# Five of eight pairs by seven products, with TensorE's matmuls in program order

## The chip, the cores and the metric

The kernel runs on one core of a Trainium2 chip. The metric is device time in microseconds, the median of several runs. The core's engines are TensorE (PE, matmuls; its weight loads are listed apart as PEld), VectorE (DVE), ScalarE (ACT) and GpSimd (POOL); SyncE (SP) issues the DMAs. Each engine takes its instructions in the order of its own queue and waits on semaphores for the others.

## The reference

A two-layer encoder trunk on x of 256 tokens by 2048 channels, in float32. Each layer is a mixer followed by a feed-forward part:

```python
x = layer_norm(DN_ALPHA * x + y, ln_mix_g[layer], ln_mix_b[layer])       # y from the layer's mixer
f = swiglu(x, ffn_w_gate[layer], ffn_w_up[layer], ffn_w_down[layer])
x = layer_norm(DN_ALPHA * x + f, ln_ffn_g[layer], ln_ffn_b[layer])

def swiglu(x, w_gate, w_up, w_down):
    return (jax.nn.silu(x @ w_gate) * (x @ w_up)) @ w_down
```

`w_gate` and `w_up` are 2048 x 5632, `w_down` is 5632 x 2048. The mixers (neighbourhood attention with a gated recurrence in layer 0, pooling with grouped-query attention in layer 1) are outside the change.

## The kernel before

**Numbers in two parts.** A float32 value is held as `hi`, rounded to the matmul's type float32r, and `lo`, the rest. `split` (L121) makes both: ScalarE casts (L122), VectorE subtracts (L123). `mm3` (L289) multiplies two such pairs by three matmuls (lo by hi, hi by hi, hi by lo) of 128x128 weights and 512 columns; the activations are the weights that are loaded, the split weight matrix streams. Tokens make two blocks of 128, the 2048 channels 16 blocks of 128.

**Loads.** `load_half` (L147) brings 512 KB of a weight matrix as `raw` and splits it into `whi` and `wlo`; in the stretch of the change there are four rooms of each. These loads have the planner's priority moved ahead by 400 instructions, so that they are made early.

**The feed-forward part.** `ffn` (L546) treats the 5632 hidden channels as 11 chunks of 512. Chunks 0 and 1 are done by `whole`. The other nine are units, nine calls of `unit` (L463) in each of the two layers, arranged in rounds:

```python
ROUNDS = (((2, 3), (0, 1)), ((4, 5), (2, 3)), ((6, 7), (4, 5)), ((8, 9), (6, 7)), ((10,), (8,)))
```

In the round ((4, 5), (2, 3)), the units 4 and 5 make gate and up of their chunks, while pieces of the down projection of chunks 2 and 3, made a round earlier, run between their products. `down_steps` (L516) is a generator, and each `next` is one piece: one half load of `w_down` and 12 matmuls into `acc`. For each of four column blocks n, the pieces go through the chunks of the round: first chunk half 0, half 1, second chunk half 0, half 1. A round of two units has 16 pieces, 8 per unit. Chunks 9 and 10 have their down projection at the layer's end.

**Seven products.** A unit computes [gate, up] for the two token blocks. Of the 16 channel blocks two neighbours form a pair p, so that a pair is a 2x2 by 2x2 block product, with 8 products done plainly. The pairs in `SEVEN` are done with 7, by Winograd's form of Strassen's method. It needs sums of blocks: those of x (`e`, `f`, `g`, `h` in `fm`) are made once a layer by `forms_of` (L417), in steps handed out by `make` (L584) after the half loads of chunk 1; those of the weights for every pair in `load_seven` (L441), which loads 1024 KB as `rs`, adds on VectorE into `z` (L452 to L454), casts and subtracts into `sh`, `sl` (four planes, two rooms) and `zh`, `zl` (one plane more, four rooms, kept until the second half of the unit). There is one room of `z` and two of `rs`.

A unit begins with two down pieces; then it transposes the two token blocks of the previous unit's y (`flips`, which call `transpose4`, L274: four transposes by TensorE, then a split into `yTh`, `yTl`, of which there are four rooms). Then come the pairs of `SEVEN`, four products each into the banks c11, c12, c22, c21, with down pieces after each by `GAPS`; a few additions on the banks (L482 to L487); and in the second half, by turns, the remaining three products of a pair in `SEVEN` and the eight of a pair in `PLAIN`. At the end silu(gate) times up makes `g`, whose transposes the next unit does. The banks `un` are a ring of four that serves the transposes and the four results.

**The order.** A planner arranges each engine's queue by the data's dependences, by the priority of program order and by a simulated time line. Splits of y and the last steps have a priority moved ahead by 1000, loads by 400. A matmul passed through `tc.keep_in_program_order` (in `mm3` with `pin`) is tied behind the TensorE instruction traced before it; in units and down pieces no matmul is.

Of the kernel before, what the change touches and what calls it, by code (L numbers as in the profile page):

```python
# [71 lines left out]
LAST = (9, 10)  # L72
SEVEN = (4, 5, 6, 7)
PLAIN = (0, 1, 2, 3)
GAPS = (2, 1, 1, 2)


@with_exitstack
def trunk(ctx: ExitStack, tc: tile.TileContext, a, out):
# [177 lines left out]
    def new_yT():  # L257
        yh = ap_.tile([P, 4, T], F32R, tag="yTh", name="yTh", bufs=4)
        yl = ap_.tile([P, 4, T], F32R, tag="yTl", name="yTl", bufs=4)
        return yh, yl  # L260

    def x_lhs(xT):
# [153 lines left out]

    def forms_of(sp, xT, out):  # L417

        n = len(SEVEN)
        xs = sp.tile([P, NT, 2 * n, P], F32, tag="rs", name="xs", bufs=2)  # L420
        fs = sp.tile([P, 4, n, P], F32, tag="z", name="fs", bufs=1)
        yield
        for t in range(NT):
            s = slice(2 * SEVEN[0], 2 * SEVEN[0] + 2 * n)
            nc.vector.tensor_tensor(xs[:, t], xT[0][t][:, s, :].bitcast(F32), xT[1][t][:, s, :].bitcast(F32), op=add)
            yield
        x11, x12, x21, x22 = (xs[:, t, e : 2 * n : 2, :] for t in range(2) for e in range(2))
        e, f, g, h = (fs[:, i] for i in range(4))
        nc.vector.tensor_tensor(e, x22, x21, op=sub)
        nc.vector.tensor_tensor(f, e, x11, op=add)  # L430
        yield
        nc.vector.tensor_tensor(g, x11, x21, op=sub)
        nc.vector.tensor_tensor(h, x12, f, op=sub)
        yield
        hi, lo = split_tile(sp, [P, 4, n, P], fs, "fm")
        for i, p in enumerate(SEVEN):
            x = lambda t, k: (xT[0][t][:, k, :], xT[1][t][:, k, :])
            e, f, g, h = (at((hi, lo), slice(None), j, i) for j in range(4))
            out[p] = {"11": x(0, 2 * p), "12": x(0, 2 * p + 1), "22": x(1, 2 * p + 1), "e": e, "f": f, "g": g, "h": h}

    def load_seven(sp, src):  # L441

        with tc.high_priority(offset=400):
            raw = sp.tile([P, 4, NCH], F32, tag="rs", name="rs", bufs=2)
            hi = sp.tile([P, 4, NCH], F32R, tag="sh", name="sh", bufs=2)
            lo = sp.tile([P, 4, NCH], F32R, tag="sl", name="sl", bufs=2)
            zh = sp.tile([P, NCH], F32R, tag="zh", name="zh", bufs=4)
            zl = sp.tile([P, NCH], F32R, tag="zl", name="zl", bufs=4)
            z = sp.tile([P, 4, NCH], F32, tag="z", name="z", bufs=1)
# [13 lines left out]
    def unit(sp, w, lhs, forms, y, down, flips):  # L463
# [5 lines left out]

        run(2)  # L470
        while flips:
            flips.pop(0)()
        b = {n: bank("un", 4) for n in ("c11", "c12", "c22", "c21")}
        edge = {}
        for i, (p, gap) in enumerate(zip(SEVEN, GAPS)):
            wt, edge[p] = load_seven(sp, w[p])
            for j, x, name in BEGIN:
                mm3(b[name], forms[p][x], wt(j), i == 0, i == len(SEVEN) - 1)
            if i == len(SEVEN) - 1:
# [9 lines left out]

        left = {n: 4 * len(PLAIN) // 2 + (n != "c22") * len(SEVEN) for n in b}  # L490

        def product(name, x, wt):
            left[name] -= 1
            mm3(b[name], x, wt, False, left[name] == 0, skip_group_check=True)

        for p, s in zip(PLAIN, SEVEN):
            hi, lo = load_half(w[s][:, 1:3])
            for i, x, name in ((0, "12", "c11"), (1, "h", "c12")):
                product(name, forms[s][x], (hi[:, i, :], lo[:, i, :]))
            product("c21", forms[s]["22"], edge[s])  # L500
            half_done()
            for n, ks in ((0, (2 * p, 2 * p + 1)), (1, (2 * p + 1, 2 * p))):
                hi, lo = load_half(w[p][:, 2 * n : 2 * n + 2])
                for tok in range(NT):
                    for kk in range(2):
                        product(f"c{tok + 1}{n + 1}", lhs(tok, ks[kk]), (hi[:, kk, :], lo[:, kk, :]))
                half_done()
# [8 lines left out]
    def down_steps(w, chunks, ys, res, start):  # L516
# [3 lines left out]
        for n in range(4):  # L520
# [8 lines left out]
            for c, ci, i in steps:  # L529
                hi, lo = load_half(w[n, 2 * c + i])  # L530
                for tok in range(NT):
                    for kk in range(2):
                        begin = (c, i, kk) == (chunks[0], 0, 0)
                        end = (c, i, kk) == (chunks[-1], 1, 1)
                        x = lhs(tok, 4 * ci + 2 * i + kk)
                        mm3(outs[tok], x, (hi[:, kk, :], lo[:, kk, :]), fresh and begin, end, skip_group_check=not fresh)
                half_done()
# [8 lines left out]
    def ffn(layer, xT, res, mix_pool, close_mix, keep, last):  # L546
# [37 lines left out]
        def make():  # L584
            with tc.issue_after(low[-1]):
                for _ in range(2):
                    if next(making[0], "end") == "end":
                        return
            later.append([1, make])

        def change_rooms():
            close_mix()
            sps.append(later_pool(stack, f"sp{layer}"))
            making.append(forms_of(sps[0], xT, forms))
            later.append([1, make])
# [494 lines left out]
    xT = new_xT()  # L1090
    yT = [new_yT() for _ in range(4)]
    with tc.tile_pool(name="wab", bufs=1) as wab:
# [33 lines left out]
    xT = layer_end(0, a["ab_out"], AB_OUT_GROUPS, yT, False)  # L1126
    yT = [new_yT() for _ in range(4)]
    with tc.tile_pool(name="cd", bufs=1, reuse_waits="tile") as mp:
# [117 lines left out]
```

## Time and profile before

| | |
|---|---|
| median of 3 runs | 2172.91 us (2172.84 to 2173.11) |
| the profiled execution's own time | 2173.93 us |
| its span in the profile | 2172.2 us |
| granted TensorE clock, mean | 0.998 |
| time of the units, by the first and last matmul into `un` | 607 to 1174 us and 1550 to 2116 us |
| DMA: read from HBM | 454.53 MB, 210 GB/s over the span |

A row of the profile names the line, engine, operation, what it writes and reads, the shapes and a count, then the busy time, the mean of one in ns, and the idle time of the engine just before, with what ended it. In a time line the first number is the start, the second the duration in microseconds. The ends of matmuls are modelled, so their starts are what counts. The chain that ended last is followed back from the last instruction; it shows which work the end hung on.

### The profile page before, as it was taken

What the parts mean: (1) busy time and instruction counts of PE and PEld (TensorE: products, weight loads), DVE (VectorE), ACT (ScalarE), POOL (GpSimd) and SP (SyncE); (2) the same over time, 40 slices, a digit from 0 to 9 for tenths busy, and PEclk for the clock granted to TensorE, in tenths of its full rate; (3) what the DMA queues carried; (4) which work ended last, traced back from release to release, by engine and by line L of the source; (5) the groups of instructions that cost most, each with busy time, mean ns of one, the idle gap of its engine ahead of it and who ended that gap; (6) DMA issues with size and microseconds to landing.
All of it is one profiled execution on the core that took longest, in us unless ns stands there. A gap on an engine that the chain in (4) does not pass through costs nothing.

```text
span 2172.2 us, 27033 instructions
## 1 busy us (share of the span) xinstructions
PE 2151.4 (99%) x9964; PEld 1791.0 (82%) x9964; DVE 1626.4 (75%) x2090; ACT 1201.6 (55%) x1614; POOL 38.0 (2%) x43
## 2 busy tenths in 40 slices
PE   9999999999999999999999999999999999999998
PEld 7888888888888888888888788888888888888886
DVE  6885688676797777877776776676877877777856
ACT  6445534555465565666565654454555666556653
POOL 0001001000000000000000000000000000000000
PEclk9999999999999999999999999999999999999999
DMA  8555545584666666766656653555766766666744
GB/s 294 163 165 176 167 143 178 190 290 141 225 235 233 228 236 233 243 234 218 233 194 205 235 201 122 206 187 185 256 230 239 241 231 224 226 231 233 241 156 174
DMA packets 119188, 458.40 MB, mean 211 GB/s; under 512 B 14480, under 2 KB 17552, under 8 KB 108560
## 3 DMA queue, kind: packets, MB, share of 16 engines
q1 hardware_dynamic: 119056, 456.68, 61.3%
q8 instruction: 78, 1.28, 0.2%
q14 instruction: 54, 0.44, 0.1%
HBM read 454.53 MB, written 2.10 MB: 210 GB/s over the span
## 4 chain that ended last, share of the span: by engine, by line
PE 95%; DMA 2%; DVE 2%; ACT 1%; issue 0%; SPq 0%; ACTq 0%; DVEq 0%
PE acc L292 51%; PE un L292 33%; PE mx L292 6%; PE mx L802 1%; PE tr L119 1%; PE un L119 1%; DVE wlo L123 1%; DMA raw<-in_down 0%; DMA raw<-in_cd_in 0%; DMA rs<-in_gu 0%; ACT whi L122 0%; PE mx L848 0%; PE mx L1060 0%; DMA raw<-in_ab_in 0%; DMA braw<-in_band 0%
## 5 line engine op out<-in xcount | busy, mean ns | idle before, releaser
L123 DVE TENSOR_TENSOR wlo<-raw,whi 128x1024 fp32r<-128x1024 f32 (+1 forms) x689 | 838.8, 1223 | 359.0 <-ACT whi L122 326.1
L122 ACT CAST whi<-raw 128x1024 fp32r<-128x1024 f32 (+1 forms) x689 | 721.1, 1051 | 687.1 <-PE acc L292 379.2
L292 PE MATMUL acc<-whi,yTl 128*128 128x512 f32 x896 | 349.7, 390 | 0.2
L292 PE MATMUL acc<-whi,yTh 128*128 128x512 f32 x896 | 348.9, 389 | 0.0
L292 PE MATMUL acc<-wlo,yTh 128*128 128x512 f32 x896 | 347.8, 389 | 0.0
L292 PE MATMUL acc<-whi,xTl 128*128 128x512 f32 x800 | 318.5, 398 | 5.3 <-ACT whi L122 5.2
L292 PE MATMUL acc<-whi,xTh 128*128 128x512 f32 x800 | 315.3, 394 | 0.0
L292 PE MATMUL acc<-wlo,xTh 128*128 128x512 f32 x800 | 312.7, 394 | 0.1
L292 PE MATMUL un<-whi,xTl 128*128 128x512 f32 x648 | 252.1, 389 | 0.0
L292 PE MATMUL un<-whi,xTh 128*128 128x512 f32 x648 | 252.1, 389 | 0.0
L292 PE MATMUL un<-wlo,xTh 128*128 128x512 f32 x648 | 245.9, 389 | 0.0
L292 PEld LDWEIGHTS acc<-whi,yTl 128*128 128x128 f32 x896 | 168.2, 188 | 35.3 <-DVE res L312 0.5
L292 PEld LDWEIGHTS acc<-wlo,yTh 128*128 128x128 f32 x896 | 168.2, 188 | 35.0
L292 PEld LDWEIGHTS acc<-whi,yTh 128*128 128x128 f32 x896 | 168.2, 188 | 34.5
L292 PEld LDWEIGHTS acc<-whi,xTl 128*128 128x128 f32 x800 | 151.2, 189 | 35.3 <-ACT whi L122 6.3
L292 PEld LDWEIGHTS acc<-wlo,xTh 128*128 128x128 f32 x800 | 151.0, 189 | 31.2 <-DVE wlo L123 0.7
L292 PEld LDWEIGHTS acc<-whi,xTh 128*128 128x128 f32 x800 | 151.4, 189 | 28.8
L292 PEld LDWEIGHTS un<-whi,xTl 128*128 128x128 f32 x648 | 121.6, 188 | 25.3
L292 PEld LDWEIGHTS un<-wlo,xTh 128*128 128x128 f32 x648 | 121.6, 188 | 25.3
L292 PEld LDWEIGHTS un<-whi,xTh 128*128 128x128 f32 x648 | 121.6, 188 | 25.2
L123 DVE TENSOR_TENSOR sl<-z,sh 128x1536 fp32r<-128x1536 f32 x72 | 126.4, 1755 | 14.4 <-ACT sh L122 13.8
L122 ACT CAST sh<-z 128x1536 fp32r<-128x1536 f32 x72 | 106.5, 1479 | 7.7 <-DVE z L453 7.7
(247 smaller groups left out, 2635.1 us busy)
## 6 DMA issues: line engine op xcount, KB each, us to landing
raw<-in_gu SPq DMA_DIRECT2D x280, 512.0 KB, 4.3
raw<-in_down SPq DMA_DIRECT2D x176, 512.0 KB, 4.3
rs<-in_gu SPq DMA_DIRECT2D x72, 1024.0 KB, 7.0
raw<-in_ab_in SPq DMA_DIRECT2D x127, 512.0 KB, 4.1
raw<-in_cd_in SPq DMA_DIRECT2D x40, 512.0 KB, 4.2
raw<-in_ab_out SPq DMA_DIRECT2D x32, 512.0 KB, 4.2
raw<-in_cd_out SPq DMA_DIRECT2D x32, 512.0 KB, 4.2
bias<-in_na_bias SPq DMA_DIRECT2D x32, 64.0 KB, 4.1
```

The source lines that it names most:

```text
L119: return nc.tensor.transpose(o, src, eye)
L122: nc.scalar.copy(hi, src)
L123: return nc.vector.tensor_tensor(lo, src, hi.bitcast(F32), op=sub).ins
L292: ins = nc.tensor.matmul(o, lhs[a], rhs[b], start=start and n == 0, stop=stop and n == 2, **more)
L802: nc.tensor.matmul(m[:, 2 * h + s, :], kk[:, h, s * P : (s + 1) * P], qq[:, h, r * P : (r + 1) * P], start=True, stop=True,)
```

## The change

- `SEVEN` has five pairs (3 to 7), and three are plain. `GAPS` gives the down pieces after each of the five: 1, 1, 1, 0, 2.
- A unit begins with a down piece, the transposes of the first token block, a down piece, those of the second block, and a third down piece.
- In the second half the pairs follow `ORDER`: 3, 0, 4, 5, 1, 6, 7, 2.
- Every matmul of a unit's pairs and of the down pieces is kept in program order.
- `forms_of` runs twice in a layer, for pairs 3 to 5 (`fm`) and 6 and 7 (`fn`).
- Room in SBUF: the rings of `yTh` and `yTl` have three rooms. A tile of their size, `fourth`, holds the mixer's fourth group of y, and in a unit `zh` and `zl` of the last two pairs; the rings of `zh` and `zl` have three rooms.

```diff
-SEVEN = (4, 5, 6, 7)
-PLAIN = (0, 1, 2, 3)
-GAPS = (2, 1, 1, 2)
+SEVEN = (3, 4, 5, 6, 7)
+GAPS = (1, 1, 1, 0, 2)
+ORDER = (3, 0, 4, 5, 1, 6, 7, 2)
...
     def new_yT():
-        yh = ap_.tile([P, 4, T], F32R, tag="yTh", name="yTh", bufs=4)
-        yl = ap_.tile([P, 4, T], F32R, tag="yTl", name="yTl", bufs=4)
+        yh = ap_.tile([P, 4, T], F32R, tag="yTh", name="yTh", bufs=3)
+        yl = ap_.tile([P, 4, T], F32R, tag="yTl", name="yTl", bufs=3)
         return yh, yl
+
+    def fourth():
+
+        return tuple(ap_.tile([P, 4, T], F32R, tag=n, name=n, bufs=1) for n in ("y4h", "y4l"))
...
-    def forms_of(sp, xT, out):
-
-        n = len(SEVEN)
+    def forms_of(sp, xT, out, seven, tag):
+
+        n = len(seven)
...
-            zh = sp.tile([P, NCH], F32R, tag="zh", name="zh", bufs=4)
-            zl = sp.tile([P, NCH], F32R, tag="zl", name="zl", bufs=4)
+            zh, zl = room or (sp.tile([P, NCH], F32R, tag=n, name=n, bufs=3) for n in ("zh", "zl"))
...
-        run(2)
-        while flips:
+        for _ in range(NT):
+            run(1)
             flips.pop(0)()
+        run(1)
         b = {n: bank("un", 4) for n in ("c11", "c12", "c22", "c21")}
-        edge = {}
+        edge, room = {}, None
         for i, (p, gap) in enumerate(zip(SEVEN, GAPS)):
-            wt, edge[p] = load_seven(sp, w[p])
+            if i == 3:
+                room = [x.rearrange("p (e a) t -> p e (a t)", e=2) for x in fourth()]
+            wt, edge[p] = load_seven(sp, w[p], room and [x[:, i - 3] for x in room])
             for j, x, name in BEGIN:
-                mm3(b[name], forms[p][x], wt(j), i == 0, i == len(SEVEN) - 1)
+                mm3(b[name], forms[p][x], wt(j), i == 0, i == len(SEVEN) - 1, True)
...
-            mm3(b[name], x, wt, False, left[name] == 0, skip_group_check=True)
-
-        for p, s in zip(PLAIN, SEVEN):
-            hi, lo = load_half(w[s][:, 1:3])
-            for i, x, name in ((0, "12", "c11"), (1, "h", "c12")):
-                product(name, forms[s][x], (hi[:, i, :], lo[:, i, :]))
-            product("c21", forms[s]["22"], edge[s])
-            half_done()
+            mm3(b[name], x, wt, False, left[name] == 0, True, skip_group_check=True)
+
+        for p in ORDER:
+            if p in SEVEN:
+                hi, lo = load_half(w[p][:, 1:3])
+                for i, x, name in ((0, "12", "c11"), (1, "h", "c12")):
+                    product(name, forms[p][x], (hi[:, i, :], lo[:, i, :]))
+                product("c21", forms[p]["22"], edge[p])
+                half_done()
+                continue
...
-                        mm3(outs[tok], x, (hi[:, kk, :], lo[:, kk, :]), fresh and begin, end, skip_group_check=not fresh)
+                        mm3(outs[tok], x, (hi[:, kk, :], lo[:, kk, :]), fresh and begin, end, True, skip_group_check=not fresh)
...
-                    if next(making[0], "end") == "end":
-                        return
+                    if next(making[0], "end") == "end":
+                        making.pop(0)
+                        if not making:
+                            return
...
-            making.append(forms_of(sps[0], xT, forms))
+            making.append(forms_of(sps[0], xT, forms, SEVEN[:3], "fm"))
+            making.append(forms_of(sps[0], xT, forms, SEVEN[3:], "fn"))
...
-    yT = [new_yT() for _ in range(4)]
+    yT = [new_yT() for _ in range(3)] + [fourth()]
```

More of the change, by code (lines that the diff above doesn't have):

```diff
@@ L423, in forms_of @@
         for t in range(NT):
-            s = slice(2 * SEVEN[0], 2 * SEVEN[0] + 2 * n)
+            s = slice(2 * seven[0], 2 * seven[0] + 2 * n)
             nc.vector.tensor_tensor(xs[:, t], xT[0][t][:, s, :].bitcast(F32), xT[1][t][:, s, :].bitcast(F32), op=add)
@@ L434, in forms_of @@
         yield
-        hi, lo = split_tile(sp, [P, 4, n, P], fs, "fm")
-        for i, p in enumerate(SEVEN):
+        hi, lo = split_tile(sp, [P, 4, n, P], fs, tag)
+        for i, p in enumerate(seven):
             x = lambda t, k: (xT[0][t][:, k, :], xT[1][t][:, k, :])
@@ L439, in forms_of, with load_seven @@
             out[p] = {"11": x(0, 2 * p), "12": x(0, 2 * p + 1), "22": x(1, 2 * p + 1), "e": e, "f": f, "g": g, "h": h}
-    def load_seven(sp, src):
+    def load_seven(sp, src, room):
         with tc.high_priority(offset=400):
@@ L488, in unit @@
             run(gap)
-        left = {n: 4 * len(PLAIN) // 2 + (n != "c22") * len(SEVEN) for n in b}
+        left = {n: 2 * (8 - len(SEVEN)) + (n != "c22") * len(SEVEN) for n in b}
         def product(name, x, wt):
             left[name] -= 1
-            mm3(b[name], x, wt, False, left[name] == 0, skip_group_check=True)
-        for p, s in zip(PLAIN, SEVEN):
-            hi, lo = load_half(w[s][:, 1:3])
-            for i, x, name in ((0, "12", "c11"), (1, "h", "c12")):
-                product(name, forms[s][x], (hi[:, i, :], lo[:, i, :]))
-            product("c21", forms[s]["22"], edge[s])
-            half_done()
+            mm3(b[name], x, wt, False, left[name] == 0, True, skip_group_check=True)
[7 more added lines that the diff above has]
+                continue
             for n, ks in ((0, (2 * p, 2 * p + 1)), (1, (2 * p + 1, 2 * p))):
@@ L1126, in trunk @@
     xT = layer_end(0, a["ab_out"], AB_OUT_GROUPS, yT, False)
-    yT = [new_yT() for _ in range(4)]
+    yT = [new_yT() for _ in range(3)] + [fourth()]
     with tc.tile_pool(name="cd", bufs=1, reuse_waits="tile") as mp:
```

## The prediction

> **What bounds the kernel now.** I read the page first (busy time, then the shares of the chain that ended last), then that chain in order of time, then busy time by stretches.
>
> ```profile
> span 2172.2 us, 27033 instructions
> PE 2151.4 (99%) x9964; PEld 1791.0 (82%) x9964; DVE 1626.4 (75%) x2090; ACT 1201.6 (55%) x1614; POOL 38.0 (2%) x43
> PE 95%; DMA 2%; DVE 2%; ACT 1%; issue 0%; SPq 0%; ACTq 0%; DVEq 0%
> PE acc L292 51%; PE un L292 33%; PE mx L292 6%; PE mx L802 1%; PE tr L119 1%; PE un L119 1%; DVE wlo L123 1%; DMA raw<-in_down 0%; DMA raw<-in_cd_in 0%; DMA rs<-in_gu 0%; ACT whi L122 0%; PE mx L848 0%; PE mx L1060 0%; DMA raw<-in_ab_in 0%; DMA braw<-in_band 0%
> ```
>
> TensorE carries 95% of the chain. A busy PE is no proof of a full one, so the spacing of matmuls comes next, from the chain, and then one unit by engine (729.58 to 793.07 us), and the later two thirds of the one before it.
>
> ```profile
> 729.58 5.45 PE acc L292 x24
> 763.15 29.92 PE un L292 x132
> 793.07 5.44 PE acc L292 x24
> ```
> ```profile
> 729.58:793.07 63.49, 63.49 (x285) 52.64 (x285) 50.31 (x53) 38.07 (x47) 0.00 (x0) 1.00 0.69 232
> 672.20:696.26 24.06, 24.06 (x109) 19.96 (x108) 17.98 (x20) 13.97 (x20) 0.00 (x0) 1.00 0.60 211
> 696.26:729.58 33.32, 33.32 (x148) 27.60 (x148) 28.54 (x30) 21.41 (x26) 0.00 (x0) 1.00 0.76 257
> ```
>
> The columns of the stretches are PE, PEld, DVE, ACT, POOL, granted clock, DMA share, GB/s. 132 matmuls in 29.92 us are 0.2267 us each. A unit has 276 of them (180 for gate and up, 96 for its eight down pieces of 12), 62.6 us, and the transposes of y; it lasts 63.5. So a unit holds no gap worth taking: only fewer matmuls shorten it, and any new wait lengthens it. VectorE stands at 50.3 of 63.5 us, 79%, but in the second half of the unit (third row) at 28.5 of 33.3.
>
> **The matmuls taken away.** The count by tile:
>
> ```profile
> L292 PE MATMUL un<-whi,xTl 128*128 128x512 f32 x648 | 252.1, 389 | 0.0
> L292 PE MATMUL un<-sh,fml 128*128 128x512 f32 x216 | 84.1, 389 | 0.0
> L292 PE MATMUL un<-sh,xTl 128*128 128x512 f32 x72 | 29.6, 411 | 0.0
> L292 PE MATMUL un<-whi,fml 128*128 128x512 f32 x72 | 28.2, 392 | 0.5 <-DVE un L484 0.5
> L292 PE MATMUL un<-zh,xTl 128*128 128x512 f32 x72 | 28.0, 389 | 0.0
> ```
>
> Each row is one of three matmuls of a product: (648+216+72+72+72)/18 = 60 products per unit in 18 units, that is 4x7+4x8. Afterwards 5x7+3x8 = 59. Three matmuls fewer per unit are 54 in all, 54 x 0.2267 = **-12.24 us**. (The Trainium skill, "TensorE: Matmul & The Clock Gate", back-to-back issue gap, measures 215.7 ns for 512 columns; by it the estimate would be -11.65. The chain has 226.7 here, and the sum uses that.)
>
> **What the fifth pair costs the other engines.** A pair by seven products replaces two loads of 512 KB and their splits by `load_seven` (1024 KB) and one 512 KB load.
>
> ```profile
> L123 DVE TENSOR_TENSOR wlo<-raw,whi 128x1024 fp32r<-128x1024 f32 x20 | 24.4, 1222 | 11.1 <-ACT whi L122 9.2 <-PE un L119 1.5
> L123 DVE TENSOR_TENSOR sl<-z,sh 128x1536 fp32r<-128x1536 f32 x4 | 7.0, 1759 | 0.9 <-ACT sh L122 0.9
> L452 DVE TENSOR_TENSOR z<-rs 128x1024 f32<-128x1024 f32 x4 | 4.9, 1222 | 0.0
> L454 DVE TENSOR_TENSOR z<-z,rs 128x512 f32<-128x512 f32 x4 | 2.8, 688 | 0.1
> L122 ACT CAST sh<-z 128x1536 fp32r<-128x1536 f32 x72 | 106.5, 1479 | 7.7 <-DVE z L453 7.7
> L451 ACT CAST sh<-rs 128x512 fp32r<-128x512 f32 x72 | 44.7, 621 | 56.0 <-DMA rs<-in_gu 30.8 <-PE un L292 22.5 <-PE acc L292 2.8
> ```
> ```profile
> 684.82 1.22 DVE L452 TENSOR_TENSOR z<-rs 128x1024 f32<-128x1024 f32 x1
> 685.96 0.68 DVE L455 TENSOR_TENSOR sl<-rs,sh 128x512 fp32r<-128x512 f32 x1
> 686.56 0.68 DVE L453 TENSOR_TENSOR z<-z,rs 128x512 f32<-128x512 f32 x1
> 688.90 1.75 DVE L123 TENSOR_TENSOR sl<-z,sh 128x1536 fp32r<-128x1536 f32 x1
> 690.57 0.69 DVE L455 TENSOR_TENSOR sl<-rs,sh 128x512 fp32r<-128x512 f32 x1
> ```
>
> Back to back, instructions on VectorE start 1.14 us apart after 1024 columns, 0.60 after 512, 1.67 after 1536. `load_seven` holds one of 1024, four of 512 and one of 1536: 5.21 us. Less one split of 1.14 it adds 4.07 per unit: 54.4 of 62.8 us, 87%. VectorE doesn't become the bound on the mean. ScalarE gains 0.62+1.48+0.62-1.05 = 1.67 us on 38.1, the DMA 0.52 MB on 14.7 (232 GB/s become 243); SP issues as many DMAs as before. All this I cost at nothing as long as it lies beside TensorE; whether it does is decided where the pairs follow each other:
>
> The pairs have two slots of `sh`/`sl`. From the end of the first pair's products to the sixth matmul of the fifth, which first reads the fifth's large `sl`, TensorE has three pieces, three pairs and five matmuls, 77 x 0.2267 = 17.5 us. VectorE owes in that time: for the third pair the two `sl` parts (2.27, its sums can be made earlier), the fourth whole (5.21), the fifth without `zl` (4.61): 12.1 us. That leaves room for four splits of a half load, where three pieces need three and some are loaded ahead (four slots). The tightest link is the fifth pair's slot: it comes free one piece and one pair (5.44 us) before its first product, and 0.62 + 1.48 + 1.75 = 3.85 us of casts and subtraction follow, read after 6.57. It fits with 2.7 us to spare if its sums are done. Bounds per unit: at best the pinned order saves the wait of the row `un<-whi,fml` (0.5 us in all), so nothing; at worst one split goes in front and costs 1.14. I take **0**, since the unit has waited for none of this so far.
>
> Rooms: `y` rings shrink from four to three. The y of unit c is written in unit c+1, into the room of c-3, whose last reading piece has run by then in every round (for the second unit of a round it is piece 14 of the 16 just ended). The rooms of `fourth` are last read ahead of the last pair's 24 matmuls and written after the next unit's three pieces. I see no wait there: 0.
>
> **The third piece ahead of the pairs.** In the first unit of rounds 1 to 4 the third piece is the first one that reads the y transposed just before it; earlier, a pair's products stood between. With TensorE in program order nothing may slip in between. This is the price of the change:
>
> ```profile
> 671.41 1.03 PE L119 MATMUL un<-ident,g 128*128 128x128 f32 x8
> 672.20 0.48 PE L292 MATMUL un<-sh,xTl 128*128 128x512 f32 x1
> 671.38 1.05 ACT L122 CAST whi<-raw 128x1024 fp32r<-128x1024 f32 x1 [1.67 <-PE acc L292]
> 672.33 1.06 ACT L122 CAST yTh<-un 128x512 fp32r<-128x512 f32 x2
> 672.46 1.23 DVE L123 TENSOR_TENSOR wlo<-raw,whi 128x1024 fp32r<-128x1024 f32 x1 [1.49 <-PE un L119]
> 673.60 1.28 DVE L123 TENSOR_TENSOR yTl<-un,yTh 128x512 fp32r<-128x512 f32 x2
> L292 PEld LDWEIGHTS un<-whi,xTl 128*128 128x128 f32 x648 | 121.6, 188 | 25.3
> ```
>
> Call 671.41 e, the end of a piece. That end also frees a slot for the next half load, so ScalarE casts `whi` first (e to e+1.02), then yTh; VectorE makes `wlo` first and starts yTl at e+2.19. One token block takes 0.68: ready at e+2.87. Afterwards, with four transposes (half of the 0.79 to 672.20) after the second piece, the third begins at e+0.40 and reaches the second token block six matmuls later, e+1.76; its first matmul needs the lo part as weights, whose load takes 0.19, so it starts at e+3.06. **1.30 us of wait, at eight places (four rounds, two layers): +10.4.** Queued behind are all of TensorE's matmuls. Bounds per place: with neither cast nor split ahead, e+0.63 (the eight end at e+1.03, four of them 0.40 earlier) + 0.53 + 0.68 + 0.19 = e+2.03, a wait of 0.3; with one more of each ahead 1.30+1.14 = 2.4. I take 1.30, since this order stands in the row.
>
> **The start of a layer's units.** `forms_of` now runs twice, for three and two pairs.
>
> ```profile
> 570.00:640.00 70.00, 69.84 (x314) 57.57 (x313) 62.65 (x69) 39.87 (x46) 0.00 (x0) 1.00 0.68 240
> L425 DVE TENSOR_TENSOR xs<-xTh,xTl 128x1024 f32<-128x1024 f32 x2 | 2.3, 1216 | 0.0
> L123 DVE TENSOR_TENSOR fml<-fs,fmh 128x2048 fp32r<-128x2048 f32 x1 | 2.3, 2291 | 1.5 <-ACT fmh L122 1.5
> L432 DVE TENSOR_TENSOR fs<-xs 128x512 f32<-128x512 f32 x1 | 0.7, 685 | 0.0
> ```
>
> Before: 2.3 + 4 x 0.69 + 2.3 = 7.4 us of VectorE; a quarter more columns and seven more starts (about 0.06 each, 2 x 0.60 less 1.14) make 9.6, +2.2; with the fifth pair's 4.07, 6.3 us more into a stretch with 7.35 idle. It fits on paper only. Between 0 and 3 us per layer, I take 1: **+2.0**.
>
> **The sum.** -12.24 + 10.4 + 2.0 = +0.2 us on the profiled span: 2172.4, and 2174.1 for the run as a whole (2173.93 before, 1.0 above the median shown of 2172.91). As a median: **2173.1**. A difference under 0.2%, 4.3 us, can't be told from none here.
>
> **Rivals.**
> 1. The y splits go ahead of the casts. Each has a place ahead of everything in the planner's order (offset 1000 against 400); against it, the row shows that a cast that is ready sooner wins. Then 8 x 0.3 = 2.4: -7.8, **2165.1**.
> 2. VectorE is late for the fifth pair. If splits of half loads stand in front of its sums for over 2.7 us, each further one costs 1.14; in the ten units whose first pieces don't wait (a wait there gives VectorE time), 11.4 more: **2184.5**, slower. For it: 28.5 busy of 33.3 us where loads are made ahead. Against it: the 12.1 of 17.5 us.
> 3. The clock falls at each of the eight waits.
>
> ```profile
> 1230.65 0.66 PE L119 MATMUL tr<-ident,res 128*128 128x128 f32 x4 [2.59 <-ACT res L344]
> 1230.00:1234.00 4.00, 3.35 (x15) 2.78 (x15) 3.04 (x7) 4.00 (x9) 0.00 (x0) 0.71 0.85 292
> 1234.00:1238.00 4.00, 4.00 (x21) 3.28 (x20) 3.25 (x8) 2.62 (x9) 0.00 (x0) 0.86 0.42 148
> ```
>
> After an idle time of 2.59 us the granted clock is 0.71 and 0.86 for 4 us each: 0.29 x 4 + 0.14 x 4 = 1.7 us lost. Eight times: 13.8 more, **2186.9**. Against it: the wait is half as long. (The same page of the Trainium skill, part 1, drops the clock after an idle window of about 3.4 us; by that none of these waits does. The trace fell after 2.59.)
> 4. The change doesn't do what it says: a transpose floats past its place. Every marked matmul is tied to the TensorE instruction traced before it, the last transpose too, so at most three transposes can move; worth nothing.
>
> **Chances.** My forecast 0.42 (its own range 2168.5 to 2178: waits of 0.85 to 1.6 us per place, 0 to 2 per layer start), rival 1 0.28, rival 2 0.19, rival 3 0.06, anything else 0.05. Of the forecast's share 0.32 lies within 0.2%, 0.05 on either side. Faster 0.05+0.28+0.01 = 0.34, same 0.32+0.03 = 0.35, slower 0.05+0.19+0.06+0.01 = 0.31. The range takes in rival 1 (2165.1 less half a layer start) and rival 2: 2164 to 2186.
>
> **What would show it.** 177 products' matmuls per unit (the five rows by tile become 522, 270, 90, 90, 90) and units without a first of a round at 62.8 us. In the first unit of rounds 1 to 4, idle time of TensorE's weight load behind yTl of about 1.3 us; 0.3 speaks for rival 1. Idle time behind `sl` in units speaks for rival 2, a granted clock below 1.00 there for rival 3. Wrong altogether would be a wait for y rooms, or idle time outside the units.

## The result, and the profile after

| | before | after |
|---|---|---|
| median of 4 runs | 2172.88 us (2172.45 to 2173.11) | 2204.85 us (2201.3 to 2209.76) |
| ratio after / before, 95% interval | | 1.0148 [1.0135, 1.016] |
| profiled execution, its span | 2173.93, 2172.2 us | 2206.51, 2204.4 us |

The change makes the kernel 32 us slower. The forecast was no change (2173.1 us, with a range of 2164 to 2186). First the page of the kernel after (span and engines), the three rows of its products by tile that the forecast named, and the waits of TensorE before and after (engine, line, what it waited for: us in total, times, longest).

```profile
span 2204.4 us, 27147 instructions
PE 2155.6 (98%) x9910; PEld 1780.2 (81%) x9910; DVE 1704.3 (77%) x2194; ACT 1223.4 (55%) x1652; POOL 36.8 (2%) x43
L296 PE MATMUL un<-whi,xTl 128*128 128x512 f32 x522 | 203.2, 389 | 0.0
```
```profile
L296 PE MATMUL un<-sh,fml x162: 389/389/395, 619.3 to 2106.0; 128*128 128x512 f32 x162
L296 PE MATMUL un<-sh,fnl x108: 387/389/628, 635.7 to 2115.2; 128*128 128x512 f32 x108
```
```profile
PE un L292 <- DVE un L484: 0.5, 2, 0.3
```
```profile
PE acc L296 <- DVE yTl L123: 12.9, 9, 4.2
PE un L296 <- DVE sl L123: 11.9, 18, 1.1
PE un L296 <- ACT sh L122: 2.4, 2, 1.2
PE un L296 <- ACT un L492: 1.0, 2, 0.8
```

The matmuls went as announced (522, and 162 + 108 = 270), but TensorE now waits 28 us in the units, where it had waited 0.5. The idle time of a row is not the whole cost: in this trace the matmul behind the one that waited comes 0.11 us late too, and the granted clock may fall. So for the accounts below I took, from the starts of all matmuls of a trace, the distance from each start to the one before less the regular one (0.227 us for 512 columns), kept what was over 0.06 us, and put it to what ended the wait. The table has four kernels; two of them come later (e9 and e15, among the experiments):

| late starts of TensorE, us (places) | before | after | e9 | e15 |
|---|---|---|---|---|
| large `sl` of the fifth pair | 0 | 14.8 (18) | 5.4 (18) | 0 |
| yTl in front of a down piece | 0 | 14.6 (9) | 6.6 (2) | 0 |
| `sh` of a pair in the first unit of a layer | 0 | 2.7 (2) | 0 | 0 |
| the additions on the banks | 0.8 (2) | 2.5 (8) | 0 | 4.6 (8) |
| `wlo` of a half load in a unit | 0 | 0 | 0 | 3.9 (6) |
| the gate product ahead of the first unit | 0 | 0.8 (1) | 0.2 (1) | 2.0 (2) |
| second and later matmuls after a wait, and low clock | 19.1 | 28.9 | 25.1 | 19.8 |
| all else (start, norms, ends of layers) | 7.1 | 6.7 | 9.8 | 8.9 |
| sum | 27.0 | 71.0 | 47.1 | 39.2 |

After less before is 44.0; with the 12.2 us of matmuls that went, 31.8 us remain, and the spans differ by 32.2. So the account closes, and the loss is in the units. The account also says where the sum of the forecast (+0.2 us) fell short: 14.8 us at `sl`, where it had 0; 4.2 more than its 10.4 at yTl; 1.5 more than its 2.0 at the start of a layer (`sh` and the gate product); 1.7 at the additions; and 9.8 for second matmuls and low clock, which it didn't have.

**The wait for the fifth pair.** The time lines of VectorE and ScalarE in the unit from 742 us (start, duration, engine, line, what is written and read), and TensorE's late start behind them:

```profile
764.77 0.68 DVE L123 TENSOR_TENSOR y4l<-z,y4h 128x512 fp32r<-128x512 f32 x1
765.37 0.68 DVE L458 TENSOR_TENSOR sl<-rs,sh 128x512 fp32r<-128x512 f32 x1
765.97 1.22 DVE L455 TENSOR_TENSOR z<-rs 128x1024 f32<-128x1024 f32 x1
767.22 0.69 DVE L456 TENSOR_TENSOR z<-z,rs 128x512 f32<-128x512 f32 x1
768.30 1.23 DVE L123 TENSOR_TENSOR wlo<-raw,whi 128x1024 fp32r<-128x1024 f32 x1 [0.39 <-ACT whi L122]
769.44 0.68 DVE L457 TENSOR_TENSOR z<-z,rs 128x512 f32<-128x512 f32 x1
770.05 1.75 DVE L123 TENSOR_TENSOR sl<-z,sh 128x1536 fp32r<-128x1536 f32 x1
```
```profile
764.49 0.62 ACT L454 CAST sh<-rs 128x512 fp32r<-128x512 f32 x1 [1.10 <-PE un L296]
767.21 1.06 ACT L122 CAST whi<-raw 128x1024 fp32r<-128x1024 f32 x1 [2.10 <-PE acc L296]
768.17 1.48 ACT L122 CAST sh<-z 128x1536 fp32r<-128x1536 f32 x1
```
```profile
771.85 0.50 PE L296 MATMUL un<-sl,fnh 128*128 128x512 f32 x1 [0.60 <-DVE sl L123]
```

The sums into `z` are not made ahead. The one room of `z` comes free with y4l of the fourth pair (764.77), so the first sum starts at 765.97. Then the queues of both engines hold a half load that TensorE needs only behind the fifth pair: its cast waits for a room until 767.21 and stands ahead of the pair's cast (768.17), its subtraction waits for that cast and stands ahead of the pair's third sum and of its `sl` (770.05).

**The wait for y.** In the first unit of rounds 2, 3 and 4 of a layer a late start of 1.10 us (0.94 of it idle time) stands at the place that was forecast, by the order that was forecast: `whi` 746.47, yTh 747.42, `wlo` 747.55, yTl 748.69 in that unit. In the first unit of a layer it is much more. TensorE, and VectorE ahead of it:

```profile
613.55 0.80 PE L296 MATMUL acc<-whi,yTl 128*128 128x512 f32 x1 [4.24 <-DVE yTl L123]
614.14 0.63 PE L296 MATMUL acc<-whi,yTh 128*128 128x512 f32 x1
```
```profile
608.27 1.75 DVE L123 TENSOR_TENSOR sl<-z,sh 128x1536 fp32r<-128x1536 f32 x1
609.94 0.68 DVE L123 TENSOR_TENSOR zl<-z,zh 128x512 fp32r<-128x512 f32 x1
610.54 1.22 DVE L123 TENSOR_TENSOR wlo<-raw,whi 128x1024 fp32r<-128x1024 f32 x1
611.68 1.22 DVE L455 TENSOR_TENSOR z<-rs 128x1024 f32<-128x1024 f32 x1
612.81 0.68 DVE L123 TENSOR_TENSOR yTl<-un,yTh 128x512 fp32r<-128x512 f32 x1
```

yTh is there at 610.4, but the end of one pair by seven (`sl`, `zl`), a half load and the first sum of the next pair stand ahead of yTl on VectorE.

### The profile page after: what moved, and what is told of

Its sections match the earlier page's. It is cut to its first block, busy times and chain, and to the rows that moved or that the text cites. A ratio compares the mean times of both kernels' runs of the same rounds, so it can differ in the third digit from the quotient of the medians.

```text
span 2204.4 us, 27147 instructions
## 1 busy us (share of the span) xinstructions
PE 2155.6 (98%) x9910; PEld 1780.2 (81%) x9910; DVE 1704.3 (77%) x2194; ACT 1223.4 (55%) x1652; POOL 36.8 (2%) x43
## 5 line engine op out<-in xcount | busy, mean ns | idle before, releaser
L296 PE MATMUL acc<-whi,yTh 128*128 128x512 f32 x832 | 325.4, 391 | 0.0
L296 PE MATMUL acc<-wlo,yTh 128*128 128x512 f32 x832 | 324.7, 391 | 0.0
L296 PE MATMUL un<-whi,xTl 128*128 128x512 f32 x522 | 203.2, 389 | 0.0
L296 PE MATMUL un<-whi,xTh 128*128 128x512 f32 x522 | 203.1, 389 | 0.0
L296 PE MATMUL un<-wlo,xTh 128*128 128x512 f32 x522 | 203.1, 389 | 0.0
L123 DVE TENSOR_TENSOR sl<-z,sh 128x1536 fp32r<-128x1536 f32 x90 | 157.9, 1754 | 19.4 <-ACT sh L122 19.3
L122 ACT CAST sh<-z 128x1536 fp32r<-128x1536 f32 x90 | 133.0, 1478 | 16.8 <-DVE z L456 16.7
L454 ACT CAST sh<-rs 128x512 fp32r<-128x512 f32 x90 | 56.1, 624 | 149.5 <-DMA rs<-in_gu 64.7
L296 PEld LDWEIGHTS un<-wlo,xTh 128*128 128x128 f32 x522 | 98.0, 188 | 20.5
L296 PEld LDWEIGHTS un<-whi,xTh 128*128 128x128 f32 x522 | 98.0, 188 | 20.5
```

The source lines that it names most:

```text
L122: nc.scalar.copy(hi, src)
L123: return nc.vector.tensor_tensor(lo, src, hi.bitcast(F32), op=sub).ins
L296: ins = nc.tensor.matmul(o, lhs[a], rhs[b], start=start and n == 0, stop=stop and n == 2, **more)
L454: nc.scalar.copy(hi[:, 0], raw[:, 0])
```

## The experiments

Two theories. **Q**, the place in the queue: each engine takes its work in a fixed order, and in the changed kernel work for later (half loads, the next unit's first pair), some of it waiting for a transfer or a room, stands ahead of what TensorE needs next. **V**, the load: VectorE has too much to do, wherever its work stands. The rival within Q was whether five pairs, program order or the third piece makes the place bad. The expectations of e1 to e8 use other letters: A (with A1, A2 and D) for single waits as Q has them, B for what is V here, C for program order. Times are medians; each ratio is to the kernel before on the same chip (2172.9 to 2173.6 us), with its 95% interval.

**Moving the parts one at a time.** In e1 both blocks of y are transposed behind the first down piece. In e2 the piece missing ahead of the fifth pair comes from the place behind the first. e3 has both. e4 leaves the changed kernel as it is but for program order.

```diff
 # e1_y_early
-        for _ in range(NT):
-            run(1)
-            flips.pop(0)()
         run(1)
+        while flips:
+            flips.pop(0)()
+        run(2)
 # e2_gap_moved
-GAPS = (1, 1, 1, 0, 2)
+GAPS = (0, 1, 1, 1, 2)
 # e4_no_pins, likewise in product() and down_steps()
-                mm3(b[name], forms[p][x], wt(j), i == 0, i == len(SEVEN) - 1, True)
+                mm3(b[name], forms[p][x], wt(j), i == 0, i == len(SEVEN) - 1)
```

> The changed kernel with both token blocks transposed after the first down piece of a unit, and two pieces behind them; all else as changed. Theory A (two separate waits: the third piece waits for yTl at the start of rounds 1 to 4, the fifth pair waits for its sl in every unit): the waits of acc behind yTl (9, 14.6 us of late starts with some 3 us of slow clock behind the longest) go, the 18 behind sl stay: 2204.9 - 16 to 18 = about 2187 to 2189. Theory B (VectorE's load as a whole is the bound, so a wait that is taken away comes back at another place): over 2198. The six waits of rounds 2 to 4 alone, 1.2 us each, if the first round's have another cause: 2204.9 - 7.3 = 2197.6.

> The changed kernel with GAPS 0, 1, 1, 1, 2: the pairs without a piece between them are the first two, whose weights are made in the unit before, and the fifth pair has a piece ahead of it. Theory A: the fifth pair's slot comes free 8.2 instead of 5.4 us ahead, its 18 waits behind sl (14.8 us, 2 us of restart, some 4 us more in the first unit of each layer) go: 2204.9 - 17 to 20 = 2185 to 2188, the waits behind yTl stay. Theory B: waits behind sl or sh of the third or fourth pair of the same length, 2200 or more.

> Both edits of the two kernels above together. Theory A: the two gains add, 2204.9 - 17 - 18 = about 2168 to 2171, below before (2172.9), what is left is the wait for the bank c21 (about 3 us) and the layers' first units. Theory B: over 2190.

> The changed kernel with the matmuls of units and down pieces free to be arranged by the planner, as before the change; five pairs, three pieces, all else as changed. Theory C (the program order is the whole cause: the planner would have filled every wait): 2161 to 2168, the saving of 12.2 us unspoiled. Theory A: the waits for yTl go, as a pair's products may come in between, the lateness of the fifth pair is shifted but not gone: 2175 to 2195. Theory B: 2195 or more.

| | us | ratio |
|---|---|---|
| e1_y_early | 2197.33 | 1.0103 [1.0087, 1.012] |
| e2_gap_moved | 2208.14 | 1.0156 [1.0141, 1.0171] |
| e3_both | 2199.17 | 1.0113 [1.0098, 1.0128] |
| e4_no_pins | 2222.37 | 1.0224 [1.0209, 1.0239] |

e1 takes the six steady waits for yTl away and is worth what its third alternative gave for them alone; those of the two first units stay, 6.3 us. e2 gives nothing: the waits for `sl` stay (15.2 us of idle time in 16). In its trace the next unit's first pair is now the one in front: its cast waits 3.13 us for its transfer and stands ahead of the fifth pair's cast. e3 is accordingly no faster than e1. e4, without program order, is slower still than the changed kernel. TensorE's largest wait there, then VectorE and ScalarE in front of the longer ones:

```profile
PE un L296 <- DVE un L490: 35.8, 16, 3.8
```
```profile
774.29 0.69 DVE L489 TENSOR_TENSOR g<-un,g 128x512 f32<-128x512 f32 x1
775.91 0.69 DVE L458 TENSOR_TENSOR sl<-rs,sh 128x512 fp32r<-128x512 f32 x1 [0.94 <-ACT sh L454]
776.52 0.69 DVE L456 TENSOR_TENSOR z<-z,rs 128x512 f32<-128x512 f32 x1
777.12 0.69 DVE L490 TENSOR_TENSOR un<-g,un 128x512 f32<-128x512 f32 x1
```
```profile
775.26 0.62 ACT L454 CAST sh<-rs 128x512 fp32r<-128x512 f32 x1 [2.49 <-DMA rs<-in_gu]
```

L489 to L493 are the additions on the banks behind the fifth pair; the second half's products into c12, c21 and c22 wait for them. Between L489 and L490 stands work of the next unit's first two pairs. The `sl` at 775.91 is the second pair's: it waits for a cast, which waits for a transfer that was issued at 768.22 and landed at 775.16. This is theory Q's picture at another place.

**Holding the half load back.** e5 queues the first half load of the plain products behind the fifth pair's cast and subtraction; in e7 that goes with y early and the sums of `forms_of` made earlier; e6 is e7 without the holding.

```diff
 # e5_hold: load_seven keeps its two long instructions
-            split(hi[:, 1:], lo[:, 1:], z[:, :3])
+            big = nc.scalar.copy(hi[:, 1:], z[:, :3]).ins
+            sub_ = nc.vector.tensor_tensor(lo[:, 1:], z[:, :3], hi[:, 1:].bitcast(F32), op=sub).ins
...
+        ahead[:] = [big, sub_]
 # and the first half load of ORDER[1] is queued behind them
+                held[0] = int(p == ORDER[1] and n == 0)
                 hi, lo = load_half(w[p][:, 2 * n : 2 * n + 2])
 # e6_forms_early (with e1)
-                    later.append([4 + tok, work])
+                    later.append([2 + tok, work])
...
-        later.append([6, change_rooms])
+        later.append([4, change_rooms])
```

> The changed kernel with one thing moved: the first half load of the first plain pair (the one whose cast and subtraction stand on ScalarE and VectorE between the fifth pair's sums and its sl) is queued behind the fifth pair's cast and subtraction. Theory A1 (that one half load makes the fifth pair late): sl of the fifth pair ends about 0.6 us sooner, of the 18 waits of 0.75 us and more some 0.2 us each is left: 2204.9 - 9 to 14 = 2191 to 2196. Theory A2 (the chain of one room of z, sums, cast and subtraction is late without it): within 3 us of 2204.9. Theory B (VectorE's load as a whole): the wait moves to the bank c21 or to the second half, 2201 or more.

> The kernel with both token blocks transposed after the first piece (2197.3), and in chunk 1 the transposes of chunk 0's y and the change of rooms two half loads earlier, so that the sums of x for the five pairs are made 5.4 us earlier. Theory D (the first unit of a layer waits because forms_of and the first pairs' weights are made too late for VectorE's queue): the two waits for yTl of together 6.6 us, the two for sh (2.7), and the slow clock behind them (about 4 us) shrink by half or more: 2185 to 2191. Rival (the planner's order puts yTl behind other work there whatever the time of forms_of): 2195 to 2199.

> The three edits together (both transposes early, the half load behind the fifth pair, forms_of early). Theories A1 and D: 2197.3 - 11 - 9 = about 2174 to 2181. Theory B (a wait removed comes back elsewhere): 2190 or more.

| | us | ratio |
|---|---|---|
| e5_hold | 2231.98 | 1.027 [1.0255, 1.0286] |
| e6_forms_early | 2198.02 | 1.0115 [1.01, 1.013] |
| e7_all | 2218.13 | 1.0205 [1.0187, 1.0223] |

In e5 the usual wait for `sl` shrinks from 0.75 to 0.18 us of late start, so the half load was its cause (in the first unit of each layer it stays at 1.23). But the kernel loses 27 us to a new wait, again at the additions. TensorE's waits in e5, then VectorE and ScalarE:

```profile
PE un L296 <- ACT un L494: 28.5, 16, 2.6
```
```profile
775.95 0.69 DVE L491 TENSOR_TENSOR g<-un,g 128x512 f32<-128x512 f32 x1
776.55 1.22 DVE L455 TENSOR_TENSOR z<-rs 128x1024 f32<-128x1024 f32 x1
777.81 0.69 DVE L458 TENSOR_TENSOR sl<-rs,sh 128x512 fp32r<-128x512 f32 x1
778.42 0.69 DVE L492 TENSOR_TENSOR un<-g,un 128x512 f32<-128x512 f32 x1
```
```profile
777.15 0.63 ACT L454 CAST sh<-rs 128x512 fp32r<-128x512 f32 x1 [2.78 <-DMA rs<-in_gu]
```

The cast of the next unit's second pair waits for its transfer as in e4. e6 gains nothing over e1 (2198.02 and 2197.33). Its sums of x are ready 2.8 us earlier (the subtraction into `fnl` starts at 585.97 instead of 588.74 us), not the 5.4 expected, and the first units' waits hardly move (5.9 for 6.3 us of idle time at yTl, `sh` the same): that the time of `forms_of` delays the first unit isn't borne out.

By their times alone, e2, e3, e4, e5 and e7 came out where the expectations put theory B, the load, and outside the ranges of the single waits. What speaks against the load is the order in the rows above, and e9 and e10 below.

**How much is the fifth pair, how much the order?** e8 is the changed kernel with four pairs. e11 is the kernel before with nothing but program order.

```diff
 # e8_four
-SEVEN = (3, 4, 5, 6, 7)
-GAPS = (1, 1, 1, 0, 2)
-ORDER = (3, 0, 4, 5, 1, 6, 7, 2)
+SEVEN = (4, 5, 6, 7)
+GAPS = (1, 1, 1, 2)
+ORDER = (4, 0, 5, 1, 6, 2, 7, 3)
 # e11_before_pins, likewise in product() and down_steps()
-                mm3(b[name], forms[p][x], wt(j), i == 0, i == len(SEVEN) - 1)
+                mm3(b[name], forms[p][x], wt(j), i == 0, i == len(SEVEN) - 1, True)
```

> The changed kernel with four pairs by seven products instead of five (SEVEN 4 to 7, GAPS 1, 1, 1, 2, ORDER 4, 0, 5, 1, 6, 2, 7, 3): program order, three pieces ahead of the pairs and the rooms as changed; 180 products' matmuls as before the change. Theory A: the waits behind sl go, those behind yTl stay (six of 1.2 us and the layers' first): 2172.9 + 8 to 14 = 2181 to 2187. Theory C (program order itself costs): 2190 or more. If the third piece's wait needs the fifth pair too: 2173 to 2177.

> The kernel before (four pairs, its own start of a unit and its own rooms), with TensorE's matmuls of units and down pieces in program order and nothing else. If program order alone cost the 32 us of e8_four, it is slower by 10 us or more (over 2183 us), with waits for yTl or for ScalarE's addition into c21. If the cost is that of the third piece ahead of y with the order, it stays at 2172 to 2178 us.

e8: 2205.13 us, 1.0148 [1.0133, 1.0163], as slow as with five. Its waits for `sl` are gone; those for yTl (12.2 us of idle time in eight) stay, and fourteen of 0.5 us for the addition into c21 come. e11: 2190.33 us, 1.0078 [1.0062, 1.0093]. Its waits:

```profile
PE un L292 <- DVE yTl L123: 12.3, 18, 2.6
```

In each of the 18 units the first pair's third product must take a bank that the transposes of y have just filled, and so waits for yTl. In the kernel before, TensorE ran on there with the second pair's products into c11 and c12 and then with a piece (737.12 and 738.50 us in one unit). So program order alone costs the kernel before 17 us. That is no fixed share of the 32: the changed kernel doesn't have these eighteen waits, and taking program order away from it (e4) makes it slower. e8, which has program order and the rest of the change (start, `ORDER`, rooms) without a fifth pair, is 15 us above e11; with the fifth pair 12.2 us of matmuls go and about as much comes in waits.

**The next unit's first pair behind the additions.** In e4 and e5 the same work stands in the way. e9, e10 and e12 queue the first pair's work behind the last additions, and the second pair's then comes behind it too: e12 with y early, e9 with y early and the half load held, e10 without program order instead.

```diff
+                    neg = nc.scalar.activation(b["c21"], g1, AF.Copy, scale=-1.0)
+                    tail[:] = [neg.ins, nc.vector.tensor_tensor(b["c22"], g1, b["c22"], op=sub).ins]
...
-            wt, edge[p] = load_seven(sp, w[p], room and [x[:, i - 3] for x in room])
+            with ExitStack() as behind:
+                for ins in tail if i == 0 else ():
+                    behind.enter_context(tc.issue_after(ins))
+                wt, edge[p] = load_seven(sp, w[p], room and [x[:, i - 3] for x in room])
```

> y early, the first half load queued behind the fifth pair, and the next unit's first pair queued behind the additions from bank to bank. Theory Q (work for later stands in the in-order queues of ScalarE and VectorE ahead of what TensorE needs next): the sl waits stay near 0.18 us as in e5_hold, and the bank waits (28 to 31 us in e5_hold and e7_all) go, since no cast that waits for a transfer stands ahead of the additions; what is left over the kernel before is the first units' yTl (6.2 to 6.6 us) and restarts: 2176 to 2183 us. Theory V (VectorE has too much to do in a unit, wherever its work stands): the wait appears at a third place, and the time stays above 2195 us.

> The changed kernel without program order on TensorE, and with the next unit's first pair queued behind the additions. Theory Q: the 38.3 us of waits for the c12 and g1 additions in e4_no_pins and the restarts behind them go; what remains is what the planner's own order leaves: 2165 to 2178 us. Theory V: over 2200 us.

> y early and the next unit's first pair behind the additions, the half load left where the change has it. Theory Q: the waits for sl (14.8 us in eighteen) stay, because their cause is the half load's cast and subtraction ahead of the fifth pair, and the small waits for c21 go: 2192 to 2197 us. If the sl waits shrink too, the pair chain's late start comes from the unit's start instead: under 2188 us.

| | us | ratio |
|---|---|---|
| e9_behind_hold | 2182.14 | 1.0036 [1.0023, 1.0049] |
| e10_behind_no_pins | 2179.91 | 1.0028 [1.0017, 1.004] |
| e12_behind | 2192.41 | 1.0096 [1.0078, 1.0113] |

The same edit takes 36 us off e7 (e9, which is e7 with it and without the earlier `forms_of`) and 42 us off e4 (e10). VectorE's work is the same as before the edit (2194 instructions, busy for 1706.8 us in e7 and 1702.9 in e9), so theory V falls as the cause of these waits. In e9 the additions follow each other, no wait for them is left, and the casts of the next unit's first two pairs come behind:

```profile
766.65 0.68 DVE L495 TENSOR_TENSOR g<-un,g 128x512 f32<-128x512 f32 x1
767.44 0.70 DVE L496 TENSOR_TENSOR un<-g,un 128x512 f32<-128x512 f32 x1
768.24 0.69 DVE L497 TENSOR_TENSOR g<-g,un 128x512 f32<-128x512 f32 x1
768.96 0.69 DVE L499 TENSOR_TENSOR un<-g,un 128x512 f32<-128x512 f32 x1
769.57 1.22 DVE L455 TENSOR_TENSOR z<-rs 128x1024 f32<-128x1024 f32 x1
```
```profile
769.50 1.13 ACT L454 CAST sh<-rs 128x512 fp32r<-128x512 f32 x2
```

e9 and e12 fell inside their ranges. No run gave the transfer an earlier start, by a third room of `rs` for instance; whether that would do as well is open.

e12, where the half load stays in front, keeps all eighteen waits for `sl` (11.9 us of idle time), as Q says. e10 ended 2 us above its range; the wait that was 35.8 us in sixteen is down to this:

```profile
PE un L296 <- DVE un L494: 5.9, 10, 1.1
```

**All together.** What is left in e9 is the first unit of a layer, the clock behind it and 5.4 us at `sl`; in e10 7.5 us of late starts at the additions, which may be the half load's place. e13 (y early), e14 (half load held) and e15 (both) are e10 with those; e16 is the kernel before with the edit on the next unit's first pair alone.

> e10_behind_no_pins with both transposes of y behind the first down piece instead of one behind each of two. If the late yTl is a matter of program order alone, TensorE already took other work in e10 and this gives nothing: 2178 to 2182 us. If the third piece ahead of y delays the split of y and with it the additions into c12 (8.75 us of waits in the first unit of each round in e10), those waits go: 2168 to 2174 us.

> e10_behind_no_pins with the first half load behind the fifth pair. Theory Q: the half load's cast and subtraction stand ahead of the fifth pair's sums in e10 too, and the additions from bank to bank follow that pair; with them behind, the waits for the additions (8.75 us in ten units) shrink to a third: 2172 to 2177 us. If TensorE then waits for the held half load itself (whi or wlo), it is 2180 us or more.

> y early, the half load behind the fifth pair, the next unit's first pair behind the additions, no program order. If the two remaining causes add, it is the fastest with five pairs: 2166 to 2173 us, equal to the kernel before or faster. If the first unit of each layer (waits of 3.6 and 3.0 us for y in e9 and the lower clock behind them) is what is left, TensorE fills those without program order and the time is the same as this; if something else is left, 2176 to 2182 us.

> The kernel before, with four pairs and its own order, and the next unit's first pair queued behind the additions. Its units have waits of 0.8 us for these additions in all, so if the queue edit only mends what five pairs broke, it stays at 2170 to 2175 us. If it would help four pairs as well, it is under 2168 us, and five pairs gain nothing.

| | us | ratio |
|---|---|---|
| e13_early_behind_np | 2176.27 | 1.0015 [1.0005, 1.0024] |
| e14_hold_behind_np | 2177.89 | 1.002 [1.0011, 1.003] |
| e15_all_np | 2173.04 | 1.0001 [0.9992, 1.0011] |
| e16_before_behind | 2171.68 | 0.9993 [0.9984, 1.0003] |

e15, with five pairs, is level with the kernel before, and so is e16 with four: the edit mends what five pairs broke and gives four pairs nothing. e13 came out between its two ranges, with the waits for the additions unchanged (7.65 against 7.47 us of late starts), so y was not their cause; the two waits for `sh` in the layers' first units (1.7 us) are gone. (The 8.75 us of the expectations holds 1.3 us of a wait for the gate product besides the 7.47.) e14 lies between its ranges too: the waits for the additions shrink from 7.47 to 4.2 us of late starts, and the held half load costs 6.7 us in eight waits for `wlo`. In e15 the 12.2 us of matmuls are paid for by other waits, 8.5 of them in the additions (0.8 in the kernel before) and `wlo` of the table above. TensorE and VectorE there:

```profile
769.61 0.49 PE L296 MATMUL un<-wlo,xTh 128*128 128x512 f32 x1 [0.50 <-DVE wlo L123]
```
```profile
763.19 1.76 DVE L460 TENSOR_TENSOR sl<-z,sh 128x1536 fp32r<-128x1536 f32 x1 [1.41 <-ACT sh L459]
764.86 2.35 DVE L123 TENSOR_TENSOR wlo<-raw,whi 128x1024 fp32r<-128x1024 f32 x2
767.13 0.69 DVE L123 TENSOR_TENSOR y4l<-z,y4h 128x512 fp32r<-128x512 f32 x1
767.74 0.68 DVE L495 TENSOR_TENSOR g<-un,g 128x512 f32<-128x512 f32 x1
768.34 1.22 DVE L123 TENSOR_TENSOR wlo<-raw,whi 128x1024 fp32r<-128x1024 f32 x1
769.47 0.69 DVE L496 TENSOR_TENSOR un<-g,un 128x512 f32<-128x512 f32 x1
```

Here VectorE runs without a gap from 763.2 us, and two things that TensorE needs at once, `wlo` and the additions, take turns. At this place, the first unit of a round, V may hold after all. But just ahead VectorE stood idle for 1.41 us until the fifth pair's cast, which on ScalarE came behind two copies for a down piece (760.53 and 761.15 us). So the place in a queue is not ruled out here either. e17 and e18 tried to cover it, by a third down piece behind the fifth pair.

```diff
 # e17_gap_last
+GAPS = (1, 0, 1, 0, 3)
 # e18_gap_last_b
+GAPS = (0, 1, 1, 0, 3)
```

> e15_all_np with the pieces between pairs at 1, 0, 1, 0, 3 in place of 1, 1, 1, 0, 2: one more down piece (12 matmuls, 2.7 us) stands behind the fifth pair in program, where TensorE waits for the additions from bank to bank. If cover is what lacks, the six waits for wlo (3.9 us) and the eight for the additions (4.6 us) go: 2164 to 2170 us. If VectorE's work in that stretch is the bound, or the planner takes the pieces earlier in any case, 2171 to 2177 us.

> As e17_gap_last, with the pieces at 0, 1, 1, 0, 3: the first two pairs follow each other, and the pair chain has the cover of a piece later. Cover theory: 2164 to 2171 us, as e17; bound by VectorE: 2171 to 2178 us; if the second pair comes late for TensorE behind the first without a piece between them, over 2178 us.

e17: 2174.2 us, 1.0005 [0.9996, 1.0014]. e18: 2179.09 us, 1.0025 [1.0016, 1.0034]. Neither covers anything, and e18's loss stands at `wlo` again (7.9 us of late starts in eight), not at the second pair, as its third alternative had it. In e17 the first matmul behind the fifth pair (766.0 us) is a product of the second half, which waits 0.6 us for the copy of c11 on ScalarE: without program order the planner had used the pieces ahead of that pair. So e17 doesn't test whether cover would help; that stays open.

## Why the prediction was wrong

**The matmuls taken away: right.** 522 and 270 of the named matmuls, and -12.2 us closes the account to 0.4 us.

**"It fits with 2.7 us to spare if its sums are done ... I take 0": this step failed.** The sums were not done. They need the one room of `z`, which the fourth pair holds to its last subtraction. In the unit shown, the pair's slot comes free at 764.5 (its first cast waited for that) and the first sum starts at 765.97; from there to the end of `sl` (771.80) 5.8 us pass, where I had counted 3.85 us of casts and subtraction. Together that is 7.3 us against the 6.57 there were. About 0.66 of the 5.8 are a half load that stands in front, 0.26 by its cast on ScalarE and 0.40 by its subtraction on VectorE, behind which the third sum comes late; with it moved back the wait is 0.18 instead of 0.75 us (e5). That is rival 2 in kind: work for a half load in front. But one split was enough where rival 2 asked for several, because the one room of `z` and the sums had used up the 2.7 us; I gave it 11.4 us in ten units, and it took 14.8 in eighteen. The amount of work was right: VectorE's busy time grew by 77.9 us (1626.4 to 1704.3), and 18 x 4.07 and 2 x 2.2 are 77.7. I had compared the work owed with the time there was (12.1 of 17.5 us), which holds only for an engine that may choose what to do next. In a fixed queue the place counts, and one instruction that waits for a room or a transfer holds everything behind it.

**The third piece ahead of the pairs: right in place and order, short in sum.** Six waits of 1.10 us stand for the 1.30 forecast; but the two first units of the layers took 4.4 and 3.5, because VectorE's queue holds parts of two pairs by seven and a half load ahead of yTl there. 14.6 us for 10.4. e1 takes the six away.

**The start of a layer: near in size, the reason not borne out.** 2.7 us for `sh` and 0.8 for the gate product stand for the 2.0 forecast, but e6 has the sums of `forms_of` 2.8 us earlier and gains nothing. That the size came near is luck as far as the runs tell.

**Rooms for y: right.** No wait for one stands in TensorE's list.

**Program order: wrong.** I priced it at the one place where I saw a matmul lose its cover. e11 shows that in the kernel before it costs 17 us with nothing else changed, at eighteen places that I hadn't seen. In the changed kernel these waits don't stand: with the third piece ahead of the pairs, the banks are free when the pairs come, and the wait is for y in the piece instead. How much of the 32 us is program order's own these runs don't say: taking it away alone loses 17 us (e4), taking it away last gains 9 (e9 to e15). The sum also left out the second matmul behind each wait.

**Rival 3** was right in part: the clock did not fall at the 1.10 us waits. It fell in layer 0 behind the long wait and once more: 18 matmuls stand 0.43 us apart instead of 0.23, which with the restart costs about 4 us.

**Is the place or the load the cause?** Order decides most of it: from the changed kernel to e15, no multiplication is put back and no work is taken from VectorE (9910 matmuls and 2194 instructions of VectorE in both), and the 32 us go. Step by step, each against its own runs of before: 32.0 after, 23.7 with y early (e1), 19.0 with the next pair behind the additions (e12, intervals overlapping e1's), 8.7 with the half load held (e9), -0.2 without program order (e15). The single cures mislead: e4 and e5, each with one of them alone, were 17 and 27 us worse than the changed kernel, because what they set free ran into the next thing that was queued too early. Why five pairs don't beat four even then is not settled: the 8.5 us at the additions and `wlo` stand where VectorE has no gap but has just waited for a cast, and no run here took work off VectorE there or moved that cast. No version beat the kernel before.

## What to carry to other kernels

When an engine that is not the bound gets more to do, don't compare its total with the time there is: write down its queue in order around the next thing the bound engine needs, and ask of each entry in front whether it may wait for a transfer or a room. Work for later that starts with a transfer belongs behind the urgent work in the queue, by an explicit order if the planner puts it in front. If one cure makes it worse, look at what the bound engine waits for then before dropping it; here two single cures lost 17 and 27 us, and four together (e15) brought the time of the kernel before back.

## What the hardware showed besides

The granted clock doesn't follow from the length of a wait alone. The stretches of the kernel after behind its two kinds of waits, layer 0 then layer 1 (us; busy time and count of PE, PEld, DVE, ACT, POOL; granted clock; DMA share; GB/s):

```profile
609.00:618.00 9.00, 4.76 (x14) 3.57 (x13) 8.12 (x10) 3.48 (x6) 0.00 (x0) 0.64 0.76 282
642.30:646.00 3.70, 3.70 (x11) 2.84 (x11) 3.70 (x6) 1.63 (x2) 0.00 (x0) 0.54 0.17 73
1569.00:1578.00 9.00, 5.89 (x27) 4.41 (x26) 7.64 (x10) 3.20 (x4) 0.00 (x0) 1.00 0.61 229
1595.00:1604.00 9.00, 6.76 (x29) 4.96 (x28) 7.20 (x10) 4.00 (x6) 0.00 (x0) 1.00 0.53 177
```

In layer 0 it fell to about half behind the wait of 4.24 us, and again at 642.3 behind two waits of 1.18 and 1.06 us (638.6 to 641.5). In layer 1 the same two waits, and one of 2.43 us with another of 0.68 ahead of them, left it at 1.00. In e9 it fell after 2.80 us in layer 1 (0.53 from 1558 to 1561 us). The Trainium skill, "TensorE: Matmul & The Clock Gate", part 1, says that activity is watched in windows of some 3.4 us that run freely and don't start anew with a kernel; that agrees with equal waits that fall out differently, but no run here shows the window itself. The rule that the forecast's rival 3 quotes, a drop after an idle window of about 3.4 us, doesn't hold here: 2.80 us were enough in e9, and 2.59 in the kernel before (0.71).
